# Loading the tenth octet's K and V by group: a linear-attention kernel on one core

## The chip, the cores and the metric

The kernel runs on one core of a Trainium2 chip. A core has five engines that run side by side and wait for one another through semaphores: TensorE (PE) multiplies and transposes, VectorE (DVE) and ScalarE (ACT) work element by element, GpSimd (POOL) and SyncE (SP) here mostly issue DMA transfers, which the core's 16 DMA engines carry out. The metric is the device time of one execution in microseconds. Before the change it is 127.2 us, the median of three runs (127.05, 127.2 and 127.61).

## What is computed

Q, K and V have 8 batches of 12 heads, 512 positions and 64 features, all fp32. With relu on Q and K, each of the 96 heads computes

```
KV   = relu(K)^T V                    (64 x 64)
ksum = sum over positions of relu(K)  (64)
out  = relu(Q) KV / (relu(Q) ksum + 1e-10)
```

Each input is 12.58 MB, so 37.75 MB are read from HBM and 12.58 MB are written.

## The kernel before

Heads are handled four at a time in a *group* (24 groups) and eight at a time in an *octet* (12 octets, `NO`, counted from 0 in the code; the tenth octet is o = 9). One group's K is 128 partitions x 16 rows x 64 features; so is its V. Q and the output go by octet.

**Loads.** The first two groups' K and V come through SP in fp32. All other loads are issued by POOL, in the order of the program, and are cast to bf16 on the way: `load_kv(o)` and then `load_q(o)` for o = 1 to 11. `load_kv` (line 93) takes one buffer for K and one for V of an octet, each with room for two groups. For o < `PAIRS` it makes two transfers, K of both groups and V of both groups (line 101, 1 MB of HBM each, 512 KB in SBUF). For the other octets it makes four of half that size, in the order K of the first group, V of the first, K of the second, V of the second (line 105). `load_q` (line 107) is one transfer of 1 MB. The pools `kin` and `vin` hold six octets each, `qin` seven, so that later loads wait on POOL until a buffer is free.

**Computation.** `prep(g)` on VectorE makes relu(K) times two masks (line 144) and half of the masked V (line 146); `prep_v` makes the other half on ScalarE (line 151) or VectorE (line 153). `mm_kv(g)` accumulates KV and the sum of K on TensorE (line 158), `evac_kv` copies it out of PSUM (line 168). `qt(o)` transposes Q (line 179) and applies relu (line 187). `denom(o)` computes the denominators and their reciprocals (lines 229 to 241). `out_t(o)` multiplies with KV (line 209) and copies (line 211), and `backs(o)` transposes back on TensorE (line 247), scales on VectorE into the output tile (line 253; called the norm below) and stores.

**Order.** The order on each engine is as written in the program; nothing is rearranged (`manual_schedule`). Iteration o of the main loop (line 305, o = 0 to 9) does, up to o = 8, the products of octet o (`kvs(o)`), then `prep` and `prep_v` of the *first* group of octet o + 1, then `backs(o - 1)`, `denom(o)`, `out_t(o)`, and only then `prep` of the *second* group of octet o + 1. In iterations 8 and 9, `kvs(o + 1)`, `qt(o + 1)` and `backs(o)` follow. The last two octets end in code written out by hand, with the last store in two halves (line 266).

**Stores.** SP issues them (line 268). Ahead of the store of octet o, as long as o + 5 is an octet, stands a tiny copy (line 261) that reads one row of K of the first group of octet o + 5. So this store, and all behind it on SP, is held until that K has landed:

```
if o + DELAY < NO:
    nc.sync.dma_start(out=scratch, in_=k_sb[2 * (o + DELAY)][0:1, 0, :])
```

For octet 4's store the K in question is that of octet 9.

Of the kernel before, what the change touches and what calls it, by code (L numbers as in the profile page):

```python
# [10 lines left out]
def kernel(  # L11
# [20 lines left out]
    NO = NG // 2  # L32
    assert NO * 8 == NH and R == 16 and RQ == 32
    DELAY = 5
    F32 = 2
    PAIRS = NO - 2

    fp32 = mybir.dt.float32
    bf16 = mybir.dt.bfloat16
# [53 lines left out]
    def load_kv(o):  # L93
        pairs = [(kin.tile([P, 2, R * D], bf16, name="k_sb"), Kr, k_sb),
                 (vin.tile([P, 2, R * D], bf16, name="v_sb"), Vr, v_sb)]
        for t, _, sb in pairs:
            for i in range(2):
                sb[2 * o + i] = t[:, i].rearrange("p (r d) -> p r d", d=D)
        if o < PAIRS:
            for t, X, _ in pairs:  # L100
# [275 lines left out]
```

## Time and profile before

| | us |
|---|---|
| median of three runs | 127.2 |
| profiled execution | 127.11 |
| its span | 125.3 |
| PE busy | 87.1 (69%) |
| DVE busy | 81.2 (65%) |
| ACT busy | 78.9 (63%) |
| POOL busy | 24.9 (20%) |

The span runs from the first to the last event of the profiled execution; about 1.8 us of its time lie outside. The page divides the span into 40 slices and gives for each the busy tenths of every engine and of the DMA engines together, and the GB/s that arrived. It lists the DMA queues (q0 is what POOL issues, q1 what SP issues), the chain of waits that ended last, and groups of instructions. A timeline row has the start and the length in us, the engine, the line, the operation with output and input, and in brackets the idle time of the engine just before and what ended it. A row of a DMA issue ends with the KB that each issue moves (counted in SBUF) and the median time in us from issue to landing.

### The profile page before, as it was taken

The page shows a single profiled execution, that of the slowest core. Times are in us where ns is not written, and L with a number is a line of the kernel's source. Part 1 is how long each engine was busy: PE and PEld are TensorE (multiplying, and loading weights), DVE is VectorE, ACT ScalarE, POOL GpSimd, SP SyncE. Part 2 cuts the span into 40 slices and gives each one's busy share as a digit, 9 for nine tenths or more (in the row PEclk, how much of TensorE's full clock was granted, in tenths as well). Part 3 has the DMA queues.
Part 4 walks back from the last instruction along what each step waited for, and adds up shares of the span by engine and source line. Part 5 has one row for each costly group of instructions (what it writes and reads, how often), then busy time and mean ns, then how long its engine had stood idle before and what let it go on. Part 6 is the DMA issues. An engine that isn't in the chain of part 4 may idle for free.

```text
span 125.3 us, 2644 instructions
## 1 busy us (share of the span) xinstructions
PE 87.1 (69%) x1075; PEld 79.7 (64%) x1075; DVE 81.2 (65%) x176; ACT 78.9 (63%) x114; POOL 24.9 (20%) x44
## 2 busy tenths in 40 slices
PE   0041096998989899894993894896698758797800
PEld 0050185997878788792992793696497556696700
DVE  2615753939798897929727916934945945988630
ACT  0241549969898997986863866667529919646400
POOL 6922132221322222112211103103111000000000
PEclk9999999599999999999599599679869999999997
DMA  3999999999999999999999999999999999999992
GB/s 141 323 279 271 212 213 211 216 207 220 207 213 210 211 219 259 292 220 264 316 213 246 337 214 213 318 267 213 329 254 216 343 239 216 339 421 424 429 392 102
DMA packets 10460, 32.67 MB, mean 261 GB/s; under 512 B 1104, under 2 KB 1104, under 8 KB 9040
## 3 DMA queue, kind: packets, MB, share of 16 engines
q0 software_dynamic: 7776, 17.83, 74.5%
q1 hardware_dynamic: 2672, 14.68, 29.2%
q8 instruction: 8, 0.13, 0.4%
q14 instruction: 4, 0.03, 0.1%
HBM read 37.75 MB, written 12.58 MB: 402 GB/s over the span
## 4 chain that ended last, share of the span: by engine, by line
DVE 32%; DMA 30%; PE 26%; ACT 4%; issue 2%; SPq 1%; DVEq 1%; ACTq 0%
DMA v_sb<-in_V_dram 22%; DVE o_sb L253 17%; PE ps_kv L158 12%; DMA kv_first<-in_V_dram 8%; PE ps_bk L247 8%; DVE kf L144 4%; PE ps_qt L179 3%; DVE vo L146 3%; ACT kvd L168 2%; DVE vo L153 2%; DVE den L237 2%; DVE own L232 2%; ACT qt L187 2%; PE ps_ot L209 1%; DVE rec L241 1%
## 5 line engine op out<-in xcount | busy, mean ns | idle before, releaser
L158 PE MATMUL ps_kv<-vo,kf 128*128 128x132 bf16 x384 | 30.7, 244 | 17.3 <-ACT vo L151 7.9
L158 PEld LDWEIGHTS <-kf 128*128 128x128 bf16 x384 | 28.3, 110 | 18.7 <-DVE vo L146 10.7
L253 DVE TENSOR_TENSOR o_sb<-ps_bk,rec 128x1024 f32<-128x1024 f32 x24 | 28.3, 1218 | 12.1 <-PE ps_bk L247 12.1
L168 ACT CAST kvd<-ps_kv 64x260 bf16<-64x260 f32 (+1 forms) x54 | 18.7, 346 | 17.3 <-PE ps_kv L158 15.1
L211 ACT COPY ot_sb<-ps_ot 128x1024 f32<-128x1024 f32 x22 | 21.9, 1014 | 7.8 <-PE ps_ot L209 7.3
L144 DVE TENSOR_SCALAR kf<-k_sb,mask 128x1024 bf16<-128x1024 bf16 x44 | 18.7, 466 | 7.8 <-DMA k_sb<-in_K_dram 7.8
L247 PE MATMUL ps_bk<-ident,ot_sb 128*128 128x128 f32 x192 | 23.0, 273 | 0.0
L187 ACT ACTIVATE qt<-ps_qt 128x1024 bf16<-128x1024 bf16 x23 | 22.4, 1028 | 0.1
L209 PE MATMUL ps_ot<-qt,kvd 128*128 128x256 bf16 x88 | 14.3, 295 | 10.6 <-DVE o_sb L253 10.6
L247 PEld LDWEIGHTS ps_bk<-ident,ot_sb 128*128 128x128 f32 x192 | 20.8, 141 | 0.0
L209 PEld LDWEIGHTS <-kvd 128*128 128x128 bf16 x88 | 8.7, 102 | 13.4 <-issue 12.3
L179 PE MATMUL ps_qt<-ident,q_sb 128*128 128x128 bf16 x192 | 16.6, 254 | 0.0
L179 PEld LDWEIGHTS <-q_sb 128*128 128x128 bf16 x192 | 15.3, 117 | 0.5
L146 DVE TENSOR_SCALAR vo<-v_sb,mask 128x1024 bf16<-128x1024 bf16 x22 | 10.6, 482 | 5.8 <-DMA v_sb<-in_V_dram 5.8
L151 ACT ACTIVATE vo<-v_sb,mask 128x1024 bf16<-128x1024 bf16 x10 | 11.5, 1154 | 2.8 <-DMA v_sb<-in_V_dram 2.7
L109 POOL DMA_DIRECT2D q_sb<-in_Q_dram x12 | 6.9, 572 | 21.5 <-PE ps_kv L158 8.0
L229 PEld LDWEIGHTS <-qt 128*128 128x128 bf16 x192 | 6.7, 96 | 5.0 <-ACT qt L187 3.7
L101 POOL DMA_DIRECT2D v_sb<-in_V_dram x9 | 6.6, 731 | 15.3 <-DMA q_sb<-in_Q_dram 9.1
L229 PE MATMUL ps_den<-kvd,qt 128*128 128x16 bf16 x192 | 7.5, 180 | 3.1 <-ACT qt L187 2.5
L101 POOL DMA_DIRECT2D k_sb<-in_K_dram x9 | 6.5, 720 | 11.8 <-DMA v_sb<-in_V_dram 7.8
L232 DVE SCALAR_TENSOR_TENSOR own<-ps_den,mask_h 128x256 f32<-128x256 f32 x12 | 5.0, 416 | 3.1 <-PE ps_den L229 3.1
L153 DVE TENSOR_SCALAR vo<-v_sb,mask 128x1024 bf16<-128x1024 bf16 x12 | 5.8, 480 | 0.0
(29 smaller groups left out, 34.1 us busy)
## 6 DMA issues: line engine op xcount, KB each, us to landing
out_dram<-o_sb SPq DMA_DIRECT2D x11, 1024.0 KB, 8.9
q_sb<-in_Q_dram POOLq DMA_DIRECT2D x12, 512.0 KB, 20.7
k_sb<-in_K_dram POOLq DMA_DIRECT2D x9, 512.0 KB, 22.3
v_sb<-in_V_dram POOLq DMA_DIRECT2D x9, 512.0 KB, 21.6
kv_first<-in_K_dram SPq DMA_DIRECT2D x2, 512.0 KB, 5.6
kv_first<-in_V_dram SPq DMA_DIRECT2D x2, 512.0 KB, 7.1
k_sb<-in_K_dram POOLq DMA_DIRECT2D x4, 256.0 KB, 19.4
v_sb<-in_V_dram POOLq DMA_DIRECT2D x4, 256.0 KB, 18.3
```

The source lines that it names most:

```text
L101: nc.gpsimd.dma_start(out=t, in_=X[2 * o:2 * o + 2].rearrange("g p f -> p g f"), single_packet=True)
L144: nc.vector.tensor_scalar(kf[g][:, :, s, :], k_sb[g], scalar1=0.0, scalar2=mask[:, 0, s:s + 1], op0=Alu.max, op1=Alu.mult)
L146: nc.vector.tensor_scalar(vo[g % NB][:, :, 0, 2:D + 2], v_sb[g], scalar1=mask[:, 1, 0:1], scalar2=None, op0=Alu.mult)
L158: nc.tensor.matmul(ps_kv[:, g % 2, 0:2 * (D + 2)].rearrange("p (t d) -> p t d", t=2), kf[g][:, r, :, :].rearrange("p s d -> p (s d)"), vo[ ...
L168: copy(kvd[o % NK][64 * c:64 * c + 64, 4 * gs.start + s:4 * gs.stop:2, c * D1:c * D1 + D1].rearrange("p (g t) d -> p g t d", t=2), ps_kv[6 ...
L179: nc.tensor.transpose(ps[:, u, :], q_sb[o][:, i * (U // 2) + u, :], ident)
L187: nc.scalar.activation(to, ps, Act.Relu)
L209: nc.tensor.matmul(ps[:, i], kvd[o % NK][:, h, 1:2 * D + 1], q[:, :, h, :], start=True, stop=True, skip_group_check=True)
L211: nc.scalar.copy(ot[o][:, :, 4 * j:4 * j + 4], ps.rearrange("p h u c -> p u h c"))
L229: nc.tensor.matmul(ps[:, u], qt_sb[o % NZ][:, u, :], kvd[o % NK][:, :, 0:2 * D1:2 * D1 - 1], start=True, stop=True, skip_group_check=True)
L247: nc.tensor.transpose(ps[:, 2 * v:2 * v + 2].rearrange("p c d -> p (c d)"), ot[o][:, 8 * j + v].rearrange("p h c -> p (h c)"), ident32)
L253: nc.vector.tensor_tensor(o_sb[:, rs], ps, rec[o][:, rs].unsqueeze(2).to_broadcast([P, 16, D]), op=Alu.mult)
```

## The change

`PAIRS` goes from 10 to 9. Octets 1 to 8 keep one transfer for K and one for V; octet 9 now has four transfers, as octets 10 and 11 had already. POOL issues 40 transfers instead of 38. Nothing moves on the other engines, and the bytes and buffers are the same.

```
@@ -33,7 +33,7 @@
     assert NO * 8 == NH and R == 16 and RQ == 32
     DELAY = 5
     F32 = 2
-    PAIRS = NO - 2
+    PAIRS = NO - 3
 
     fp32 = mybir.dt.float32
     bf16 = mybir.dt.bfloat16
```

More of the change, by code (lines that the diff above doesn't have):

```diff
@@ L35 @@
     F32 = 2
-    PAIRS = NO - 2
+    PAIRS = NO - 3
     fp32 = mybir.dt.float32
```

## Prediction

> **What bounds the kernel now.** I read the page first, for the slices in time and the DMA queues:
>
> ```profile
> span 125.3 us, 2644 instructions
> ...
> DMA  3999999999999999999999999999999999999992
> GB/s 141 323 279 271 212 213 211 216 207 220 207 213 210 211 219 259 292 220 264 316 213 246 337 214 213 318 267 213 329 254 216 343 239 216 339 421 424 429 392 102
> ...
> q0 software_dynamic: 7776, 17.83, 74.5%
> ...
> HBM read 37.75 MB, written 12.58 MB: 402 GB/s over the span
> ```
>
> The DMA engines are at 90% or more in every slice but the first and the last. The GB/s row seems to say otherwise, around 212 in many slices and 420 only near the end, but it counts what arrives: loads are cast from fp32 to bf16 on the way, so a load slice of 212 has read 424. The 50.33 MB of reads and writes at the 424 of a late slice would take 118.7 us of the 125.3. Two stages bear that out, one from 57.4 to 84.9 us (loads in pairs, with three stores), one from 84.9 to 110.1 us (mostly loads in groups, with three stores); the DMA view of each gives:
>
> ```profile
> q0 software_dynamic: 1899, 4.18, 79.5%
> q1 hardware_dynamic: 528, 3.15, 28.8%
> ```
> ```profile
> q0 software_dynamic: 1636, 3.74, 77.2%
> q1 hardware_dynamic: 510, 3.07, 30.3%
> ```
>
> Doubling q0 for the cast: (2 x 4.18 + 3.15) MB / 27.5 us = 419 GB/s, and (2 x 3.74 + 3.07) / 25.2 us = 419 GB/s. The same rate, whether a load is a pair or a group.
>
> The chain of waits tells another story, and it is the one that a reader would follow first. Its longest piece is a load, and the stretch around its end shows whom it holds up:
>
> ```profile
> 59.76 26.95 DMA v_sb<-in_V_dram
> ```
> ```profile
> 81.63 0.48 DVE L153 TENSOR_SCALAR vo<-v_sb,mask 128x1024 bf16<-128x1024 bf16 x1
> ...
> 84.20 0.88 DVE L144 TENSOR_SCALAR kf<-k_sb,mask 128x1024 bf16<-128x1024 bf16 x2 [2.09 <-DMA k_sb<-in_K_dram]
> ...
> 84.31 1.91 PE L247 MATMUL ps_bk<-ident,ot_sb 128*128 128x128 f32 x16
> ...
> 86.73 0.49 DVE L146 TENSOR_SCALAR vo<-v_sb,mask 128x1024 bf16<-128x1024 bf16 x1 [1.65 <-DMA v_sb<-in_V_dram]
> ...
> 87.13 2.35 DVE L253 TENSOR_TENSOR o_sb<-ps_bk,rec 128x1024 f32<-128x1024 f32 x2
> ```
>
> This is the iteration o = 8 (octets counted from 0). VectorE idles 2.09 us for K of octet 9 and 1.65 us for its V, exactly the two loads that the change splits. Everything after 87.13 on that chain is computation. So the chain says that the wait can be shortened; the DMA rows say that the end is set by bytes. Which of them holds is decided at the end of the span.
>
> **The end.** The stores of octets 6 to 11, with the median time from issue to landing of, in turn, the store of octet 10 and the two half stores of octet 11; then the DMA share (last but one number) of two windows:
>
> ```profile
> L268 SPq DMA_DIRECT2D out_dram<-o_sb x5: 332/409/532, 103.8 to 115.6; - x5
> L266 SPq DMA_DIRECT2D out_dram<-o_sb x2: 332/332/333, 119.1 to 120.2; - x2
> ```
> ```profile
> out_dram<-o_sb SPq DMA_DIRECT2D x1, 1024.0 KB, 6.0
> ```
> ```profile
> out_dram<-o_sb SPq DMA_DIRECT2D x1, 512.0 KB, 3.7
> ```
> ```profile
> out_dram<-o_sb SPq DMA_DIRECT2D x1, 512.0 KB, 3.8
> ```
> ```profile
> 119.00:121.00 2.00, 0.00 (x0) 0.00 (x0) 1.21 (x2) 0.00 (x0) 0.00 (x0) 1.00 0.94 391
> 121.00:123.00 2.00, 0.00 (x0) 0.00 (x0) 0.00 (x0) 0.00 (x0) 0.00 (x0) 1.00 0.91 365
> ```
>
> Landings: 115.6 + 6.0 = 121.6, 119.1 + 3.7 = 122.8, 120.2 + 3.8 = 124.0. The halves land 1.2 us apart, and 0.52 MB in 1.2 us is 437 GB/s: back to back, at the full rate. The last stores queue behind one another, and issuing them earlier makes them wait longer. What a perfectly fed end could save is the idle share of the two windows: 2 x 0.06 + 2 x 0.09 = 0.30 us on the mean engine. A landing needs the last engine, which sees the even 1.2 us steps; so of these 0.30 us I count none.
>
> **The change, part by part.**
>
> *Issues on POOL.* Two issues of line 101 become four of line 105, in the order K, V, K, V, still ahead of octet 9's Q:
>
> ```profile
> 54.46 0.56 POOL L109 DMA_DIRECT2D q_sb<-in_Q_dram  x1 [3.92 <-PE ps_kv L158]
> 56.90 0.70 POOL L101 DMA_DIRECT2D k_sb<-in_K_dram  x1 [1.88 <-DVE vo L146]
> 59.76 0.71 POOL L101 DMA_DIRECT2D v_sb<-in_V_dram  x1 [2.16 <-DVE own L232]
> 64.58 0.56 POOL L109 DMA_DIRECT2D q_sb<-in_Q_dram  x1 [4.12 <-PE ps_kv L158]
> ...
> 84.69 0.53 POOL L105 DMA_DIRECT2D k_sb<-in_K_dram  x1 [4.44 <-issue]
> ...
> 93.20 0.53 POOL L105 DMA_DIRECT2D v_sb<-in_V_dram  x1 [2.90 <-DMA k_sb<-in_K_dram]
> 94.67 0.53 POOL L109 DMA_DIRECT2D q_sb<-in_Q_dram  x1 [0.94 <-PE ps_qt L179]
> ```
>
> 4 x 0.53 - (0.70 + 0.71) = +0.71 us of POOL, hidden: POOL idles 1.9 to 4.1 us before each of these, and a load is issued long before it lands. Here are the times to landing of the seven rows above, in their order:
>
> ```profile
> q_sb<-in_Q_dram POOLq DMA_DIRECT2D x1, 512.0 KB, 24.7
> ```
> ```profile
> k_sb<-in_K_dram POOLq DMA_DIRECT2D x1, 512.0 KB, 27.3
> ```
> ```profile
> v_sb<-in_V_dram POOLq DMA_DIRECT2D x1, 512.0 KB, 26.9
> ```
> ```profile
> q_sb<-in_Q_dram POOLq DMA_DIRECT2D x1, 512.0 KB, 24.9
> ```
> ```profile
> k_sb<-in_K_dram POOLq DMA_DIRECT2D x1, 256.0 KB, 18.5
> ```
> ```profile
> v_sb<-in_V_dram POOLq DMA_DIRECT2D x1, 256.0 KB, 13.5
> ```
> ```profile
> q_sb<-in_Q_dram POOLq DMA_DIRECT2D x1, 512.0 KB, 15.8
> ```
>
> So Q8 lands at 79.2, K9 at 84.2, V9 at 86.7, Q9 at 89.5, octet 11's first K at 103.2, its last V at 106.7 and Q11 at 110.5. The shortest queue in front of a load is 13.5 us. Without that cover the 0.71 us would be paid. The change shortens the queue only while octet 9's halves stand in it; I estimate 10 us at the least (13.5 with two of its loads halved). Cost: 0.
>
> *The transfers.* The bytes are the same. Octet 11's three steps from the first K to the last V take 106.7 - 103.2 = 3.5 us, 1.17 us per half; V9 lands 2.5 us after K9, 1.25 us per half. A half costs no more than half a pair; the difference of 0.08 us either way is the reading's grain. Bounds for two more transfers: -0.2 to +0.2 us. I take 0, by the two stage rates. Their completions add 32 small packets to 7776 (18 pairs x 256 + 8 groups x 128 + 12 Q x 128 + 38 issues x 16 = 7776), within the bound.
>
> *What comes earlier.* From Q8 at 79.2 to K9 at 84.2 is 5.0 us for 1 MB, with a store beside it. K's first half lands between 80.4 (1.25 us at the full rate) and 81.7 (half of 5.0); VectorE is busy until 81.63 + 0.48 = 82.1, so its 2.09 us wait goes. The first half of V has then the place of K's second half: at most 84.2. Line 146 follows, and 0.40 us on (86.73 to 87.13) VectorE is ready for the norm at 84.6. What is late next is TensorE: the first eight transposes of line 247 end at 84.31 + 1.91 / 2 = 85.3. The norm starts at 85.3 and not 87.13: 1.85 us, the most that computing can gain here.
>
> *What comes later.* Line 261 holds the store of octet 4 until octet 9's first K is there; it is released 2.5 to 3.8 us earlier, and its 2.5 us of data can then stand before Q9, which lands at 89.5 + 2.5 = 92.0 at worst. TensorE wants Q9 and Q11 at these rows:
>
> ```profile
> 93.55 1.06 PE L179 MATMUL ps_qt<-ident,q_sb 128*128 128x128 bf16 x16
> ...
> 112.34 1.06 PE L179 MATMUL ps_qt<-ident,q_sb 128*128 128x128 bf16 x16
> ```
>
> 93.55 - 1.85 = 91.7 and 112.34 - 1.85 = 110.5: the lead may lose some 0.3 us at Q9 and none at Q11, which keeps its 110.5, the bytes ahead of it being the same. Computation ends 1.5 to 1.85 us early, and the stores of octets 9 to 11 enter a queue that is full.
>
> *Sum.* Against the profiled execution of 127.11 us (span 125.3 and 1.8 around it): POOL 0, transfers 0, computing -1.85 off the path, end 0: 127.1. That execution is 0.09 under the median, so 127.2. Bounds -0.30 - 0.2 and +0.2, with the runs' own spread (127.05 to 127.61): 126.6 to 127.7.
>
> A page's rule speaks against the change. The Trainium skill, "DMA: Bandwidth & Descriptors", section "Rules for kernel authors", wants at least 1 MiB per DMA, and its section on the anatomy of one DMA fits a fixed 2.0 us to each; two more transfers would by that be +4.0 us as an estimate, 131.2. The equal 419 GB/s of the two stages disagrees as long as the queue is full.
>
> **The rivals.**
>
> *The chain is right.* If the end follows the last norm, 1.85 us go: 125.3. For it: 3.7 us of waits on just these loads. Against it: the 1.2 us steps of the last landings. Chance 0.13.
>
> *Mixing stores with loads costs (slower).* When the first store meets the loads, the window from 45 to 50 us gives:
>
> ```profile
> q0 software_dynamic: 263, 0.71, 81.5%
> q1 hardware_dynamic: 87, 0.45, 23.0%
> ```
>
> (2 x 0.71 + 0.45) / 5 = 374 GB/s; against 419 that is 5 x (1 - 374/419) = 0.54 us lost. Octet 4's store, released early, falls close behind octet 3's and meets four short loads. If both meetings lose 0.54 us: +1.1, 128.3. It decides as soon as loss reappears, since a loss on a full queue is never made up. Against: the two stages with three stores each show none. Chance 0.14.
>
> *A transfer's own time shows.* A half store takes 3.8 us to land, of which 1.2 is its step, so 2.6 is its own. If octet 9's loads run out of queue, two of these make +5.2: 132.4. It needs a queue under 3.8 us; the shortest is 13.5. Chance 0.03 (the skill's rule above would act here).
>
> **How the numbers follow.** My case has 0.70. Below 0.5% (0.64 us) no measurement of this kernel can tell a change. Faster 0.12 and slower 0.18 are the rivals, with 0.01 moved for the spread of runs. The likeliest case's own range is 126.6 to 127.7; to leave out no more than 0.16 (the chain and the own-time rival) the range takes in the mixing: 126.5 to 128.4.
>
> **What would show it.** Norm of iteration 8 at 85.3 (chain of my case) with the K wait gone; the scratch copy of octet 4's store before 82; last norm about 118.4 instead of 120.2, last landings still at 122.8 and 124.0, with longer times to landing (5 us or more for the halves); load stages at 419 GB/s. I am wrong if the halves' times to landing stay at 3.8 and the landings move left (the chain), or if a window after 80 falls under 400 GB/s (mixing).

## Result and profile after

The changed kernel takes 126.7 us (median of five executions, 126.56 to 126.82) against 127.26 us for the kernel before (five, 127.05 to 127.61). The ratio is 0.9944, with a 95% interval of 0.9916 to 0.9972: faster by 0.56% (the medians differ by 0.56 us, 0.44%). The forecast was 127.2 and no change; the range of 126.5 to 128.4 holds the time, but the direction was missed. The profiled execution took 126.59 us, 0.52 less than the one before, and 0.5 of that is in the span. Of all executions reported here one, of 130.53 us in a kernel with idle matmuls, fell in a slower state with a clock of 0.92, and it is left out.

```profile
span 124.8 us, 2646 instructions
...
q0 software_dynamic: 7808, 17.83, 74.5%
```

The 32 packets and two instructions more are the two additional issues. The timeline of VectorE in iteration 8, after the change, with TensorE's transposes for the norm:

```profile
82.66 0.88 DVE L144 TENSOR_SCALAR kf<-k_sb,mask 128x1024 bf16<-128x1024 bf16 x2 [0.88 <-DMA k_sb<-in_K_dram]
83.90 0.49 DVE L146 TENSOR_SCALAR vo<-v_sb,mask 128x1024 bf16<-128x1024 bf16 x1 [0.36 <-DMA v_sb<-in_V_dram]
85.64 2.35 DVE L253 TENSOR_TENSOR o_sb<-ps_bk,rec 128x1024 f32<-128x1024 f32 x2 [1.25 <-PE ps_bk L247]
```
```profile
84.56 1.91 PE L247 MATMUL ps_bk<-ident,ot_sb 128*128 128x128 f32 x16
```

The waits for K and V fall from 2.09 and 1.65 us to 0.88 and 0.36, and TensorE is late next, as forecast. The norm starts at 85.64 instead of 87.13. Now the end, after the change: the issues of the last stores, and the times to landing of the two halves.

```profile
L268 SPq DMA_DIRECT2D out_dram<-o_sb x5: 332/408/532, 103.4 to 113.7; - x5
L266 SPq DMA_DIRECT2D out_dram<-o_sb x2: 332/332/332, 117.2 to 118.3; - x2
```
```profile
out_dram<-o_sb SPq DMA_DIRECT2D x1, 512.0 KB, 5.5
```
```profile
out_dram<-o_sb SPq DMA_DIRECT2D x1, 512.0 KB, 5.6
```

The halves are issued 1.9 us earlier (117.2 and 118.3 instead of 119.1 and 120.2), take 1.8 us longer, and land at 122.7 and 123.9 instead of 122.8 and 124.0. The lead of the computation has bought 0.1 us in this execution. The other 0.4 us lie behind the last landing: 125.3 - 124.0 = 1.3 us before, 124.8 - 123.9 = 0.9 us after. I call this stretch the *closing*; the forecast had no term for it. In it the engines wait for one another at line 371, the end of the program. SyncE's waits there (us in total, how often, the longest), before and then after:

```profile
SPq L371 <- PEq L371: 1.0, 2, 0.5
```
```profile
SPq L371 <- PEq L371: 0.7, 2, 0.5
```

The view names TensorE's sequencer (PEq), but the step that comes late is GpSimd's. These are its first two semaphore steps at that line (with the starts of the first and the second at the end), before and then after:

```profile
L371 POOLq EVENT_SEMAPHORE  x2: 17/17/17, 124.2 to 124.6; - x2
```
```profile
L371 POOLq EVENT_SEMAPHORE  x2: 17/17/17, 124.1 to 124.2; - x2
```

In the trace's records the second starts 0.42 us behind the first before, and 0.08 us after. That is 0.33 us of the closing; a GpSimd step behind it takes 157 ns before and 93 ns after.

And queue q14, which fetches instructions, in the window from 120 to 126 us, before and after, and then in the window from 90 to 117 us after (before, q14 has no packet there):

```profile
q14 instruction: 2, 0.02, 0.8%
```
```profile
q14 instruction: 1, 0.01, 0.3%
```
```profile
q14 instruction: 1, 0.01, 0.1%
```

One fetch of 8 KB has moved. Before, the two late ones begin at 122.4 and 125.3 us; after, the last two begin at 98.3 and 122.0. The fetch at 125.3 begins only as the span ends, so nothing in the closing waits for its data:

```profile
q14 instruction: 1, 0.01, 3.9%
```

This is the window from 125.3 to 126 us before; from 124 to 125.3 q14 has no packet. Only POOL has more instructions than before; so the first suspicion was that POOL's stream of instructions is cut for fetching in another place, and that its pause lies at the cut.

### The profile page after: what moved, and what is told of

It is laid out like the page before. It is cut to its first block, busy times and chain, and to the rows that moved or that the text cites. A ratio compares the mean times of both kernels' runs of the same rounds, so it can differ in the third digit from the quotient of the medians.

```text
span 124.8 us, 2646 instructions
## 1 busy us (share of the span) xinstructions
PE 84.2 (67%) x1075; PEld 76.8 (62%) x1075; DVE 81.2 (65%) x176; ACT 78.8 (63%) x114; POOL 26.1 (21%) x46
## 4 chain that ended last, share of the span: by engine, by line
DVE 32%; DMA 30%; PE 22%; ACT 6%; issue 2%; SPq 1%; DVEq 1%; ACTq 0%
DMA v_sb<-in_V_dram 22%; DVE o_sb L253 15%; PE ps_kv L158 11%; DMA kv_first<-in_V_dram 8%; PE ps_bk L247 6%; DVE kf L144 5%; ACT kvd L168 3%; DVE vo L146 3%; PE ps_qt L179 3%; DVE vo L153 2%; DVE den L237 2%; DVE rec L241 2%; DVE own L232 2%; ACT qt L187 2%; ACT vo L151 1%
## 5 line engine op out<-in xcount | busy, mean ns | idle before, releaser
L158 PE MATMUL ps_kv<-vo,kf 128*128 128x132 bf16 x384 | 30.1, 240 | 18.9 <-ACT vo L151 8.0
L158 PEld LDWEIGHTS <-kf 128*128 128x128 bf16 x384 | 27.3, 107 | 20.5 <-DVE vo L146 10.8
L209 PE MATMUL ps_ot<-qt,kvd 128*128 128x256 bf16 x88 | 13.5, 283 | 10.4 <-DVE o_sb L253 10.2
L179 PE MATMUL ps_qt<-ident,q_sb 128*128 128x128 bf16 x192 | 14.8, 238 | 0.0
L146 DVE TENSOR_SCALAR vo<-v_sb,mask 128x1024 bf16<-128x1024 bf16 x22 | 10.7, 484 | 5.6 <-DMA v_sb<-in_V_dram 5.6
L179 PEld LDWEIGHTS <-q_sb 128*128 128x128 bf16 x192 | 13.5, 108 | 0.5 <-DMA q_sb<-in_Q_dram 0.2
L101 POOL DMA_DIRECT2D v_sb<-in_V_dram x8 | 5.7, 718 | 11.5 <-DMA q_sb<-in_Q_dram 7.6
L101 POOL DMA_DIRECT2D k_sb<-in_K_dram x8 | 5.6, 704 | 9.3 <-DMA v_sb<-in_V_dram 5.5
L105 POOL DMA_DIRECT2D k_sb<-in_K_dram x6 | 3.4, 568 | 15.9 <-DMA k_sb<-in_K_dram 8.0
```

What stands on the lines that cost most here:

```text
L146: nc.vector.tensor_scalar(vo[g % NB][:, :, 0, 2:D + 2], v_sb[g], scalar1=mask[:, 1, 0:1], scalar2=None, op0=Alu.mult)
L158: nc.tensor.matmul(ps_kv[:, g % 2, 0:2 * (D + 2)].rearrange("p (t d) -> p t d", t=2), kf[g][:, r, :, :].rearrange("p s d -> p (s d)"), vo[ ...
L179: nc.tensor.transpose(ps[:, u, :], q_sb[o][:, i * (U // 2) + u, :], ident)
L209: nc.tensor.matmul(ps[:, i], kvd[o % NK][:, h, 1:2 * D + 1], q[:, :, h, :], start=True, stop=True, skip_group_check=True)
```

## The experiments

Two theories stood against each other. By the *closing theory* 0.3 to 0.4 us of the gain come from POOL's two more instructions, whatever they do. By the *lead theory* the gain is the earlier computation. The runs were taken in three comparisons, each beside the kernel before, which had medians of 127.29, 127.1 and 127.41 us there; a ratio is to the one beside the run.

**Two idle instructions instead of the split.**

```
     for o in range(1, NO):
         load_kv(o)
         load_q(o)
+    for i in range(2): nc.gpsimd.memset(pad[:, i:i + 1], 0.0)
```

(`pad` is a new tile of two columns; the line that makes it is left out here.)

> The kernel before, with two tiny GpSimd memsets behind the last load, so that POOL has as many instructions as in the changed kernel, and no load is split. Closing theory (0.3 to 0.4 us of the gain lie after the last landing, in POOL's closing steps, which depend on where its instruction stream is cut for fetching): span minus last landing falls from 1.3 to 0.9 us, time 126.8 to 126.9. Lead theory (the gain is the 1.9 us by which the computation is early and the last stores are queued sooner): nothing changes, 127.2 to 127.3, last landing at 124.0, closing 1.3 us.

Measured: 126.92 us, ratio 0.9985 (0.9968 to 1.0003), twelve executions from 126.51 to 127.67. In the profile the halves are issued at 118.6 and 119.8; the second lands 4.0 us later, at 123.8, and the span ends at 124.7: a closing of 0.9.

```profile
span 124.7 us, 2646 instructions
```
```profile
SPq L371 <- PEq L371: 0.7, 2, 0.5
```

The closing came out as that theory said, and the median 0.37 us below the 127.29 of the kernel before in the same comparison. But the executions spread so far that the interval still reaches 1.

**One idle instruction**, with `range(1)` in the same place:

> The kernel before with one tiny GpSimd memset behind the last load. If one instruction is enough to bring the fetch forward: closing 0.9 us, time 126.9. If it takes two: closing 1.3 us, 127.3. Runs spread over 1 us either way, since the computation has no lead.

Measured: 126.79 us, ratio 0.9997 (0.9973 to 1.002), closing 124.9 - (119.9 + 4.1) = 0.9 us. One instruction is enough. The ten executions fall in two groups, six from 126.64 to 126.83 and four from 127.53 to 127.71, which is why the ratio says nothing.

**The split without more instructions.** Octet 9 in groups, octet 10 in pairs, so that POOL has 38 issues as before:

```
-        if o < PAIRS:
+        if o < PAIRS - 1 or o == PAIRS:
```

> Octet 9 in groups as in the changed kernel, but octet 10 in pairs, so that POOL has the 38 issues of before. Lead theory: the norm of iteration 8 starts at 85.6 as in the changed kernel, the lead of 1.9 us mostly stays, time 126.6 to 126.8. Closing theory: the lead is worth 0.1 us, the closing is back at 1.3 us, time 127.1 to 127.2.

Measured: 127.18 us, ratio 0.999 (0.9974 to 1.0006), twelve executions from 126.96 to 127.34. Two late fetches, the long wait, and a span of 125.3:

```profile
SPq L371 <- PEq L371: 1.0, 2, 0.5
```
```profile
q14 instruction: 2, 0.02, 0.9%
```

The second half is issued at 119.5 and lands 4.6 us later, at 124.1: the closing is 1.2 to 1.3. So the split alone does not shorten it. Some of the lead goes here to octet 10, whose paired V VectorE waits for:

```profile
96.52 0.49 DVE L146 TENSOR_SCALAR vo<-v_sb,mask 128x1024 bf16<-128x1024 bf16 x1 [0.48 <-DMA v_sb<-in_V_dram]
```

The same kernel **with the two idle instructions**:

> Octet 9 in groups, octet 10 in pairs, and the two tiny GpSimd memsets behind the last load: the early computation and POOL's instruction count of the changed kernel, with two loads fewer. Two-part theory (0.4 us from the closing, and the rest from computation that runs ahead of the store queue and so hides stretches at half TensorE clock): 126.6 to 126.8, closing 0.9 us, runs within 0.5 us of one another. If the closing depended on the loads and not on the instruction count: 127.1 to 127.2, as without the memsets.

Measured: 126.69 us, ratio 0.9961 (0.9942 to 0.9981), eleven of twelve executions from 126.59 to 126.89 and one at 127.20.

```profile
span 124.9 us, 2646 instructions
```
```profile
SPq L371 <- PEq L371: 0.6, 2, 0.5
```

These two kernels differ by two tiny memsets on an idle engine, and their medians by 0.49 us; they were taken in different comparisons, and by the ratios it is 0.37 us. The second half was issued at 120.2 in this execution, so it had no lead over the kernel before, and landed 3.8 us later at 124.0; the time is still that of the changed kernel. This pair decides for the closing theory. In all thirteen traces the two steps of GpSimd at line 371 start 0.42 to 0.44 us apart where POOL has the instruction count of before (four traces), and 0.08 us apart where it has one to four instructions more (nine traces).

By the Trainium skill, "Runtime: NRT & Kernel Launch", section "Instruction fetch mechanics", an engine's instructions are fetched block by block through a DMA queue while it works, and the cost of crossing into the next block is mostly hidden. The traces agree in that the time is not longer but shorter where the fetch that moves lies inside the span (at 94.7 us in the last kernel); where POOL's pause lies in the closing, they show 0.33 us that are not hidden. That this pause is such a crossing is inferred: before, the fetch begins 0.7 us behind its end.

**One step further**, `PAIRS = NO - 4`:

> One step further: octets 8 to 11 in groups, 42 issues. Lead theory: if earlier computation is what pays, iteration 7 starts its norm 1.5 to 1.9 us earlier too, but iteration 8 then waits for the same bytes, so about as the changed kernel, 126.5 to 126.7. Closing theory: also 126.6 to 126.7 if the stream is cut in the same place for four more instructions; a closing of 1.3 us again (127.1) if it is cut elsewhere. In both, load stages stay at 419 GB/s.

Measured: 126.68 us, ratio 0.9954 (0.9929 to 0.9979), closing 124.9 - (118.8 + 5.2) = 0.9 us. Two more issues change nothing more.

**What the lead is worth: the queue taken away.** The stores of octets 7 and 8 are left out, in the kernel before (first) and in the changed one:

```
-        nc.sync.dma_start(out=Ov, in_=o_sb)
+        if o not in (7, 8): nc.sync.dma_start(out=Ov, in_=o_sb)
```

> The kernel before without the stores of octets 7 and 8 (their output is left unwritten), so that 2.1 MB or 5 us of queue are gone at the end. Two-part theory: the last landing is then set by the last norm and a half store's own time of 2.5 to 3 us: last half issued at 120.2, landing at 122.7 to 123.2, time 125.8 to 126.3, so only about 1 us less for 5 us of bytes. If bytes set the end even so: 122.2.

> The changed kernel without the stores of octets 7 and 8. Two-part theory: the lead of 1.9 us shows in full once the queue is gone, with the 0.4 us of the closing: 2.0 to 2.4 us less than the kernel before without these stores, 123.5 to 124.2. If bytes set the end even so: the same as that kernel but for the closing.

Measured: 127.13 us for the kernel before without these stores (ten executions, 126.49 to 127.8; ratio 1.0, 0.9977 to 1.0024) and 125.25 us for the changed one (four, 124.87 to 126.22; 0.9867, 0.9829 to 0.9905). The issues and landings of the halves, first in the kernel before without the stores, then in the changed one:

```profile
L266 SPq DMA_DIRECT2D out_dram<-o_sb x2: 332/332/332, 119.4 to 120.5; - x2
```
```profile
out_dram<-o_sb SPq DMA_DIRECT2D x1, 512.0 KB, 2.6
```
```profile
out_dram<-o_sb SPq DMA_DIRECT2D x1, 512.0 KB, 3.7
```
```profile
L266 SPq DMA_DIRECT2D out_dram<-o_sb x2: 332/332/332, 117.2 to 118.4; - x2
```
```profile
out_dram<-o_sb SPq DMA_DIRECT2D x1, 512.0 KB, 2.7
```
```profile
out_dram<-o_sb SPq DMA_DIRECT2D x1, 512.0 KB, 3.7
```

With 2.1 MB fewer to move, the median of the kernel before is not lower, though four of its ten executions (126.49 to 126.74) lie below the lowest of the whole kernel beside it (126.78). Its last half still takes 3.7 us to land, with no other octet's store ahead of it. I had expected 2.5 to 3 and about 1 us less. So of the 3.8 us of the kernel before at most 0.1 was a queue behind other octets; the first half, with 3.7 us there and 2.6 here, did stand in one. Computation (120.2 + 3.7 = 123.9) and queue (123.9 in the changed kernel) ended together. The changed kernel has 1.9 us between the two. Without the two stores its median is 1.88 us lower, less than the 2.0 to 2.4 that I forecast; some 0.4 of that is the closing (1.5 us in the first profile, 1.0 in the second), so the medians show about 1.5 us of the lead.

**The lead eaten up.** 24 more idle matmuls ahead of the last octet's products, in the changed kernel:

```
-    idle(5, o + 1)
+    for n in (5, 8, 8, 8): idle(n, o + 1)
```

> The changed kernel with 24 more idle matmuls ahead of the last octet's products: about 24 x 0.107 = 2.6 us, of which 0.6 lie in a wait, so the last two half stores are issued some 1.9 to 2.0 us later, at 119.1 and 120.2 as before the change. Lead theory: the gain is gone, 127.2. Closing theory: the last landing moves by 0.1 us, the closing stays at 0.9, time 126.7 to 126.8.

Measured: 127.8 us, ratio 1.0024 (0.9999 to 1.0049), eleven executions from 126.72 to 128.24. Neither theory said so, because the delay came out longer: the halves were issued at 120.5 and 121.6.

```profile
L266 SPq DMA_DIRECT2D out_dram<-o_sb x2: 332/332/333, 120.5 to 121.6; - x2
```
```profile
out_dram<-o_sb SPq DMA_DIRECT2D x1, 512.0 KB, 3.7
```

The last lands at 121.6 + 3.7 = 125.3. The halves were issued 1.4 us later than in the kernel before, and the last landing came 1.3 us later. The part of the delay that I had not counted lay ahead of the idle matmuls, in the clock. Here is the stretch from one norm to the next (octets 8 and 9) in the changed kernel, and then in this one; the last but two number is the granted clock:

```profile
93.60:102.80 9.20, 6.53 (x90) 5.76 (x89) 6.14 (x12) 6.35 (x10) 0.53 (x1) 1.00 1.08 267
```
```profile
93.50:104.30 10.80, 8.13 (x91) 7.37 (x90) 6.15 (x13) 7.34 (x11) 0.83 (x2) 0.84 1.09 259
```

The same matmuls (and one more at the window's edge) lie in a stretch 1.6 us longer, and that goes with a clock of 0.84; from 100.0 to 103.4 us it is 0.50. Such stretches fall at other places from execution to execution: in the two traces of the kernel before, the last with a clock of 0.50 ahead of the end lies from 89.7 to 93.1 us and from 88.5 to 91.9 us.

**A smaller delay, with and without the lead.** 12 more idle matmuls (`for n in (5, 6, 6)`), in the changed kernel and in the kernel before with the two idle instructions:

> The changed kernel with 12 more idle matmuls ahead of the last octet's products: 12 x 0.107 = 1.3 us, of which 0.6 lie in a wait, so the last two half stores are issued some 0.7 us later, at about 117.9 and 119.0. Two-part theory: a half store takes 3.7 to 3.8 us to land on its own and the queue ends at 123.9, so any issue up to 120.2 costs nothing: 126.7, as the changed kernel. If the 1.9 us of lead act directly on the time: 127.3 to 127.4.

> The same 12 idle matmuls in the kernel before with two GpSimd memsets, which has the short closing but no lead. Two-part theory: its last half is issued at 119.8 to 120.2 without the idle matmuls, so 0.7 us more go past the point at which the queue hides them: last landing 124.3 to 124.7, time 127.4 to 127.6, against 126.9 without. If that kernel had slack too: 126.9.

Measured: 126.7 us for the changed kernel (eight executions, 126.53 to 126.9; ratio 0.9932, 0.9906 to 0.9959), unchanged as forecast. In its profile a stretch of low clock (0.86 from 92.7 to 104.2 us) and the idle matmuls together had used up the lead, and it cost nothing:

```profile
L266 SPq DMA_DIRECT2D out_dram<-o_sb x2: 332/332/332, 119.1 to 120.2; - x2
```
```profile
out_dram<-o_sb SPq DMA_DIRECT2D x1, 512.0 KB, 3.7
```

Without the lead: 127.08 us (eleven executions, 126.57 to 128.13; ratio 0.9981, 0.9952 to 1.0011). That is less than the forecast 127.4 to 127.6; in the profiled execution the halves went out at 119.0 and 120.1, just in time. Beside each other, with the same delay and the same short closing, the kernel with the lead is 0.38 us faster by the medians; the intervals overlap from 0.9952 to 0.9959. That the delay costs anything without the lead is not shown: the ratios with and without the 12 idle matmuls are alike (0.9981 and 0.9985).

**The kernel before once more**, for a second trace:

> The kernel before once more, for a second trace: closing 1.3 us again with two late instruction fetches, last half issued between 119.5 and 121 by where the stretches at half TensorE clock fall, landing 3.7 to 3.8 us later or at 124.0, whichever is later.

Measured: 127.09 us. The last half was issued at 119.8 and landed 4.2 us later, at 124.0; the span ends at 125.3, a closing of 1.3 us, with two late fetches again.

```profile
q14 instruction: 2, 0.02, 0.7%
```

## Why the prediction was right and wrong

**The step that failed: the sum lacked a term.** It put the end at 0 and let the span end with the last landing. The 1.3 us between the two were not looked at, and 0.4 of the 0.52 us that the profiled executions differ by lie there. The change part by part costed POOL's two more issues as engine time, 0.71 us hidden, and that was right; that their number shortens POOL's pause at line 371 from 0.42 to 0.08 us was not considered. The closing could have been read before, from a landing and the span; what would become of it could not. Why the pause goes stays open, with the instruction fetch as the likely reason. That 126.7 lies in the range is luck: its lower part stood for idle DMA time at the end and for a bound on the transfers, not for this.

**The last landing held in one execution, its reason only half.** It moved from 124.0 to 123.9. But I read the even 1.2 us steps of the landings as a queue that held every store. The runs without two stores show that the last half's time to landing has 3.7 us without that queue: the queue and the computation ended together. Hence the kernel before had no slack, and what delays computation beyond this in an execution shows in its time. That is the second term that I gave as 0. The medians put it at 0.1 to 0.4 us (126.92 and 126.79 with idle instructions alone, 126.7 with the split; 127.08 and 126.7 with 12 idle matmuls), but their intervals overlap, so its size is not shown. The scatter shows it more plainly: 126.83 to 128.23 in 29 executions of the kernel before, 126.51 to 127.67 in 12 with the idle instructions, 126.56 to 126.82 in 5 of the changed kernel and 126.53 to 126.9 in 8 with a delay added to it. That stretches of low clock make the late executions is suggested by the profiles that have such stretches, and by the mean clock of each execution: in the 29 of the kernel before, the four above 127.7 us have 0.915 to 0.929, and the seven at 0.945 or more stay at 127.43 or below. But one of 127.05 us has 0.928 too, and no trace of the latest executions exists, so it is not shown for them.

**The steps that held.** The norm of iteration 8 was forecast at 85.3 and came at 85.64; the last norm at 118.4, and came to its end at 118.3; the halves' time to landing over 5 us, and it was 5.5 and 5.6. The load stages of the changed kernel, from 57.4 to 84.9 and from 84.9 to 110.1 us:

```profile
q0 software_dynamic: 1929, 4.19, 79.6%
q1 hardware_dynamic: 528, 3.15, 28.7%
```
```profile
q0 software_dynamic: 1615, 3.70, 76.2%
q1 hardware_dynamic: 518, 3.14, 31.2%
```

These are 419 and 418 GB/s, so two more transfers cost nothing that can be measured and neither slower rival came about: no mixing loss, no transfer's own time. The first half of K landed later than the 80.4 to 81.7 that I gave (the copy ahead of octet 4's store went out at 82.65, not before 82), so the wait for K shrank to 0.88 us and did not go. TensorE was later still, so it cost nothing.

**The chain rival** was right that the computation gains 1.9 us and wrong about the time: the last landing is at 123.9, because the bytes ahead of it end no earlier.

## What to carry to other kernels

Read the end of a span in three parts: the last issue with its transfer's own time, the queue, and the stretch behind the last landing; a change is worth what it takes from the latest of the first two, plus what it does to the third. Where computation and queue end together, a lead of one need not show in a single profile, but here it went with a narrower spread of many executions. Before a gain of half a per cent is put down to a change's purpose, try the same number of idle instructions without it.

## What was not expected of the hardware

A single idle GpSimd instruction took 0.4 us off the closing: it is 1.2 to 1.5 us in the traces whose POOL has the instruction count of before (both of that kernel, octet 9 alone split, and the one without two stores), 0.9 to 1.0 us in those with one to four instructions more. A fetch of 8 KB of instructions, at the very end of the span in the first and inside it in the others, goes with that. That the fetch belongs to POOL's stream is inferred from what moves it; no view names its engine.

A store of 0.5 MB took 2.6 us to land and the next, 1.1 us behind it, 3.7 us, with no other octet's transfer in the queue. The packets show where the difference lies. The second store's data begin at about 121.5 us, when the first's end; 15 of the 16 DMA engines are done with them by 122.94, and one sends its last three packets until 123.76. The DMA share (last but one number) behind 122.95 is less than one engine of 16:

```profile
122.95:123.80 0.85, 0.00 (x0) 0.00 (x0) 0.00 (x0) 0.00 (x0) 0.00 (x0) 0.50 0.04 10
```

Just ahead of these three packets, from 122.64 to 122.95, lies one of q14's fetches. The same stands in the changed kernel without the stores (fetch to 120.81, last packets to 121.63) and in the one with 24 idle matmuls (to 124.03 and 124.84). So about 0.8 of the 3.7 us are one engine's; that the fetch holds it up is inferred, since the records name no engine for a packet.
